# Picking the first pair's rows in one row of eight, and asking for four weight pieces ahead of the gate products

## The chip, the core and the metric

One core of a Trainium2 chip runs the whole program. The metric is the device time of one execution in microseconds, the median of three runs. Engines: TensorE (PE; its weight loads are shown as PEld), VectorE (DVE), ScalarE (ACT), GpSimd (POOL) and SyncE (SP), which only issues transfers.

## What is computed

A decoder layer for 512 tokens of 1024 channels in float32: three token mixers (pooling, latent attention, cross-attention into a memory), gated, projected and added to the residual, then a mixture of experts and a last norm. The change lies in the mixture of experts:

```
g_idx = argmax(h2 @ w_rg + b_rg)                 # 1 of 4 groups
top_p, top_i = top_k(softmax(e_logits[g_idx]), 2)  # 2 of its 8 experts
weights = p_g * top_p / sum(top_p)
for each expert e, on its tokens xb:
    a = silu(xb @ w_gate_e[e]) * (xb @ w_up_e[e])  # 1024 -> 256
    y = a @ w_down_e[e]                            # 256 -> 1024
out = x + sum over a token's experts of weight * y ; out = rms_norm(out)
```

Each of the 32 experts has 3.1 MB of weights, and all of them are read once.

## The kernel before

The first two thirds of the program (to about 527 us) compute the mixers, the projection and the router. Then the 32 experts are worked off as 16 pairs (`Pair`, `PP[0]` to `PP[15]`). A pair has 128 slots, 64 for each expert; `onehot` makes its matrix P (token by slot, a 1 where the token sits in the slot), and `by_slot` multiplies P with a few columns per token, which gives these columns by slot. With the token numbers that yields the row numbers for the gather (`place`, `fetch`: an indirect DMA on POOL from the copy `xd` of the rows in DRAM into `XG`, of which there are two, XB and a tile called y); with `INF` it yields the weights of the slots (`info`).

The rows of a pair are needed with channels on the partitions, as eight blocks k of 128 channels by 128 slots. For pairs 1 to 15 they are gathered and then turned (`turn_x`, four blocks at a time). The first pair doesn't wait for a gather: `pick_x` multiplies the rows in SBUF (`ACC`) with P, four matmuls a block, and ScalarE copies the block to SBUF with the norm's gain. In `up(k)` block k meets the gate and up weights of both experts (four passes on PE, 128x512 in the trace, into the bank `gu`); `turn` and `down` follow one pair later.

The order on every engine is the one in which the program is written; each pair goes through a list of steps. For the first pair that is `SEQ0`:

```
"X0 b1 X1 b2 X2 U0 X3 U1 X4 U2 X5 U3 X6 U4 X7 U5 j0 o U6 j1 x0 U7 L x1 j2 j f"
```

Xk is `pick_x(k)`; bn is the slot product with token numbers and the gather of pair n; Uk is `up(k)`; jn is `info` of pair n (without a number, of pair 3), o the `onehot` of pair 3, f its gather; xc is `turn_x(c)` of the next pair; L is told of below. Four blocks in a row share one PSUM bank (tag xe, two banks); the slot products have one bank (tag at).

Weights come in 192 pieces of 512 KB through a ring of 40 places made of tiles that earlier stages leave free (`place`, `load_piece`). After every second U, `used(2)` says that two places are free, and SP then issues the next two pieces (`load`); `down` frees four. SP issues in the order of the program, and a request waits until its place is free and until a transfer eight before it has landed. Places 36 to 39 of the ring are the tile `ac`, the place of `ACC`: x's rows lie there until the last pick. Their pieces (the down weights of pair 2) are left out by `load` and asked for in step L, behind U7. At pair 9 (`SC`) the rows, to which pairs 0 to 8 have added their results in DRAM (`xo`, indirect DMAs on POOL), are read back into SBUF (L1363), and later pairs add theirs there (`combine`, matmuls L1177 and additions L1179).

Of the kernel before, what the change touches and what calls it, by code (L numbers as in the profile page):

```python
# [9 lines left out]
F32 = mybir.dt.float32  # L10
# [3 lines left out]
AF = mybir.ActivationFunctionType  # L14
# [8 lines left out]
KD = 8  # L23
# [14 lines left out]
P_MIX, P_MEM, P_Q, P_KV, P_PS, P_GB, P_FFN, P_END = 0, 8, 16, 19, 21, 25, 49, 57  # L38
# [3 lines left out]
def trunk_and_moe(ctx, tc, a, out):  # L42
    nc = tc.nc
    v, s, g, pe = nc.vector, nc.scalar, nc.gpsimd, nc.tensor
# [34 lines left out]
    def nm(b):  # L79
        n[0] += 1  # L80
        return f"{b}{n[0]}"

    def at(dt=F32, shape=(128, 512)):
        return UA.tile(list(shape), dt, tag="u", name=nm("u"), bufs=8)
# [17 lines left out]
    def mt(dt=F32, shape=(128, 512)):  # L102
        return G2.tile(list(shape), dt, tag="m", name=nm("m"), bufs=6)
# [4 lines left out]
    def bank(p, tag, bufs, shape=(128, 512)):  # L108
        return p.tile(list(shape), F32, tag=tag, name=nm(tag), bufs=bufs)

    def mmb():
        return bank(PA, "mm", 4)

    K = cst.tile([128, C_END], F32, name="K")
    PR = cst.tile([128, P_END], F32, name="PR")
# [223 lines left out]
    ps = mmb()  # L339
# [157 lines left out]
    for h_ in range(XHEADS):  # L497
# [3 lines left out]
        ps = mmb()  # L501
        mm3(ps[:, :MEM], kterms(w, ms))
        tick()
        t = mt()
# [28 lines left out]
    for h_ in range(XHEADS):  # L533
# [22 lines left out]
        ps = mmb()  # L556
# [54 lines left out]
    scale = 192.0 ** -0.5  # L611
# [23 lines left out]
    for d in range(KD):  # L635
        w = WS.use("w_bpm", d)
        res = []
        for j, y in enumerate((yp, ym)):
            ps = mmb()
# [39 lines left out]
    def load_piece(i):  # L679
        e, c = pieces[i]  # L680
        ts = place(i)
        n_ = 2 // len(ts)
        for t in ts:
            if len(ts) == 2:
                t = t.unsqueeze(1)
            sync.dma_start(t, a["w_e"][e, :, c * T:(c + n_) * T].rearrange("p (k f) -> p k f", f=T))
            W[e][c:c + n_] = [t[:, j] for j in range(n_)]
            c += n_
# [12 lines left out]
    def used(n_):  # L701
        ring["used"] += n_
        load(max(min(ring["used"] + RING, 3 * RING - 4), ring["used"] + RING - 4))
# [96 lines left out]
    for h_ in range(HEADS):  # L800
        for op in SEQ:
            k, i = op[0], op[1:]
# [21 lines left out]
            elif k == "V" and h_ % 2:  # L824
                p = (h_ + 1) // 2
# [97 lines left out]
    def row_major():  # L923
        return W1.tile([128, 8, T], F32, tag="ac", name=nm("ACC"), bufs=1).rearrange("p (t a) b -> p t (a b)", t=4).rearrange("p t (a b) -> p t a b", b=128)

    ACC = row_major()
# [72 lines left out]
    L = R1[:, :, 0:36]  # L999
# [4 lines left out]
    def bc(x, *shape):  # L1004
        while len(x.shape) < len(shape):
            x = x.unsqueeze(len(x.shape))
        return x.broadcast_to(list(shape))
# [31 lines left out]
    tokr = cst.tile([128, 4, 2], F32R, name="tokr")  # L1039
# [12 lines left out]
    PC = Scope("pc", space=PSUM).p  # L1052
# [8 lines left out]
    def ut(shape, dt=F32):  # L1061
        return W1.tile(list(shape), dt, tag="e1", name=nm("u"), bufs=18) if extra[0] else at(dt, shape)

    class Pair:
# [25 lines left out]
        def pick_x(self, k):  # L1090

            if k % 4 == 0:
                self.xps = bank(PC, "xe", 2, (128, 4, 128))
                self.xe.append(ut((128, 4, 128)))
            for t in range(4):
                pe.matmul(self.xps[:, k % 4], lhsT=ACC[:, t, k], rhs=self.P[:, t].bitcast(F32), start=t == 0, stop=t == 3)
            s.activation(self.xe[-1][:, k % 4], self.xps[:, k % 4], AF.Copy, scale=PR[:, P_FFN + k:P_FFN + k + 1])

        def turn_x(self, c):
            ps = bank(PC, "xe", 2, (128, 4, 128))  # L1100
# [72 lines left out]
    def combine(i, q):  # L1173
        t, hs = i // 2, slice((i % 2) * 512, (i % 2) * 512 + 512)
        cb = bank(PC, "cb", 1) if i % 2 else bank(PC, "xe", 2)
        for j in range(2):
            pe.matmul(cb, lhsT=q.PT[:, t], rhs=q.y[j][:, hs], start=j == 0, stop=j == 1)  # L1177
        dst = ACC[:, t].rearrange("p a b -> p (a b)")[:, hs]
        v.tensor_tensor(dst, dst, cb, op=OP.add)  # L1179

    def pairs(x):
        return x.rearrange("p t (b a) -> p t a b", b=2)
# [5 lines left out]
    PP = [Pair(p, pairs(code)[:, :, p], None, scattered=p < SC) for p in range(NP)]  # L1188
    for q in PP[:3]:
        q.onehot()  # L1190


    v.tensor_reduce(sm[:, 6], t4, axis=AX, op=OP.add)
    v.scalar_tensor_tensor(sm[:, 9], sm[:, 8], 1.0, sm[:, 6], op0=OP.add, op1=OP.mult)
# [3 lines left out]
    v.tensor_tensor(t32, A1, bc(sm[:, 10], 128, 4, 32), op=OP.mult)  # L1198
    v.tensor_tensor(Wd, A2, bc(sm[:, 11], 128, 4, 32), op=OP.mult)
    v.tensor_tensor(Wd, Wd, t32, op=OP.add)  # L1200
    tok = K[:, C_TOKID:C_TOKID + 4]
    INF = cst.tile([128, 4, NE // 2, 8], F32R, name="INF")

# [9 lines left out]
    def tiles():  # L1213
        mps = bank(PC, "y", 2, (128, 32))
        for t in range(4):
            pe.matmul(mps, lhsT=KB[:, B_ONES:B_ONES + 128], rhs=Ab[:, t], start=t == 0, stop=t == 3)
        v.reduce_max(nt[:, 0:16], mps.rearrange("p (b a) -> p a b", b=2), axis=AX)
        v.reduce_max(nt[:, 16:17], nt[:, 0:16], axis=AX)
        v.tensor_scalar(flag, nt[:, 16:17], float(CAP), None, op0=OP.is_gt)
# [57 lines left out]

    SEQ0 = "X0 b1 X1 b2 X2 U0 X3 U1 X4 U2 X5 U3 X6 U4 X7 U5 j0 o U6 j1 x0 U7 L x1 j2 j f".split()  # L1280
    SEQM = "o U0 c U1 j c U2 c t c U3 x0 D n U4 w c U5 c x1 c U6 f c U7".split()
    SEQ14 = "U0 c U1 c U2 c t c U3 x0 D U4 w U5 c c x1 c c U6 c c U7 c c".split()
    SEQL = "t D U0 U1 U2 U3 I c c U4 s0 c c U5 s1 c c U6 s2 U7 r3 c c s3 r4 S0 S1 t S2 S3".split()
# [5 lines left out]
    def wide():  # L1289
        return W0.tile([128, 2, T], F32, tag="e0", name=nm("e"), bufs=6).rearrange("p a b -> p (a b)")  # L1290

    for p, q in enumerate(PP):
        q.wts = [W[2 * p], W[2 * p + 1]]
        last = p == NP - 1
        if p == NP - 2:
            gf = XG[0]
            g.dma_start(gf, a["final_g"].broadcast_to([128, D]))
        if last:

            q.rw = fs[:, 0, 3:4]  # L1300
            v.tensor_tensor(q.rw, q.rs, q.wt, op=OP.mult)
            junk, o = wide(), wide()
            ys = []
        for op in (SEQ0 if p == 0 else SEQL if last else SEQ14 if p == NP - 2 else SEQM):
            n_ = int(op[1]) if len(op) > 1 else p + 3
            if op[0] == "U":
                q.up(n_)
                if n_ % 2:
                    used(2)
            elif op == "c" and todo:  # L1310
                todo.pop(0)()
            elif op[0] == "X":
                q.pick_x(n_)
            elif op[0] == "b":
                PP[n_].fetch(PP[n_].by_slot(tokr, 2)[:, 0:1])
            elif op[0] == "x" and not last:
                PP[p + 1].turn_x(n_)
            elif op == "w" and SC <= p < NP - 1:
                q.where()
            elif op == "L":  # L1320
                PP[0].place(PP[0].it[:, 6:7])
                for i in range(RING - 4, RING):
                    load_piece(i)
            elif op == "n" and p == 1:
                tiles()
            elif op[0] in "ojf" and n_ < NP:
                if op[0] == "o":
                    PP[n_].onehot()
                if op[0] == "j":
                    PP[n_].info()  # L1330
                if op[0] == "f":
                    PP[n_].fetch(PP[n_].it[:, 6:7])
            elif op == "I":
                order.__exit__(None, None, None)
                with tc.If(nc.values_load(flag[0:1, 0:1], min_val=0, max_val=1) > 0):
                    extra[0] = True
                    overflow()
                    extra[0] = False
                order = tc.manual_schedule()
                order.__enter__()  # L1340
            elif op[0] == "s":
                s.activation(junk, tok_rows(n_), AF.Square, accum_out=fs[:, n_, 0:1])
            elif op[0] == "r":
                ts = slice(0, 3) if n_ == 3 else slice(3, 4)
                s.activation(fs[:, ts, 1], fs[:, ts, 0], AF.Sqrt, bias=eps[:, 0:1], scale=1.0 / D)
                if n_ == 4:
                    v.reciprocal(fs[:, 0:3, 2], fs[:, 0:3, 1])
            elif op[0] == "S":
                if n_ == 0:
                    ys += [bank(PC, "y", 2) for hf in range(2)]  # L1350
                for hf in range(2):
                    pe.matmul(ys[hf], lhsT=q.P[:, n_].bitcast(F32), rhs=tok_rows(n_)[:, hs[hf]], start=n_ == 0, stop=False)  # L1352
            elif op == "t" and last and ys:
                q.turn()
            elif op == "t":
                PP[p - 1].turn()
            elif op == "D":
                PP[p - 1].down()
                used(4)
                if p == SC:  # L1360
                    ACC = row_major()
                    for t in range(4):
                        g.dma_start(ACC[:, t].rearrange("p a b -> p (a b)"), xo[t * 128:(t + 1) * 128])  # L1363
                if p > SC:
                    todo += [lambda i=i, q=PP[p - 1]: combine(i, q) for i in range(8)]
# [9 lines left out]
    f = fs[:, 4]  # L1375
# [103 lines left out]
```

## Time and profile before

| | |
|---|---|
| median of 3 runs | 800.81 us (800.29 to 801.99) |
| the profiled execution, its own time | 801.2 us |
| its span (first to last instruction) | 799.4 us |
| mean granted clock of TensorE | 0.992 |
| PE busy | 775.8 us, 97% |
| transfers | 164.17 MB, 205 GB/s on average |

The profile is a list of what each engine did and when. The page divides the span into 40 slices of 20 us; the expert stage is slices 27 to 40. A busy share tells how much of a stretch an engine worked, an idle time in square brackets behind an instruction who ended the wait before it. The trace puts a matmul's line on PE (its duration holds the way through the array, so that neighbours overlap) and its weight load on PEld. A float32 product of the picks shows as two passes, so that a pick of four matmuls has eight loads; SPq and POOL DMA lines are the issuing of transfers, not their movement.

### The profile page before, as it was taken

What the parts mean: (1) busy time and instruction counts of PE and PEld (TensorE: products, weight loads), DVE (VectorE), ACT (ScalarE), POOL (GpSimd) and SP (SyncE); (2) the same over time, 40 slices, a digit from 0 to 9 for tenths busy, and PEclk for the clock granted to TensorE, in tenths of its full rate; (3) what the DMA queues carried; (4) which work ended last, traced back from release to release, by engine and by line L of the source; (5) the groups of instructions that cost most, each with busy time, mean ns of one, the idle gap of its engine ahead of it and who ended that gap; (6) DMA issues with size and microseconds to landing.
All of it is one profiled execution on the core that took longest, in us unless ns stands there. A gap on an engine that the chain in (4) does not pass through costs nothing. (4 is left out here: it accounts for less than half of the span.)

```text
span 799.4 us, 10154 instructions
## 1 busy us (share of the span) xinstructions
PE 775.8 (97%) x3743; PEld 523.8 (66%) x3743; DVE 366.3 (46%) x673; ACT 303.6 (38%) x623; POOL 277.1 (35%) x169
## 2 busy tenths in 40 slices
PE   7999999999999999999999999999999999999995
PEld 3778888888887888788888888854333333333432
DVE  5669684243446134677774433142212122454544
ACT  6254354343345544655653321122232223122223
POOL 3156676543241689522222924230212122000000
PEclk8999999999999999999999999999999999999998
DMA  6532333322221322211115379988999999999963
GB/s 220 186 106 106 106 106 132 132 80 80 80 79 43 110 89 82 64 47 57 54 54 211 132 277 342 374 289 307 392 378 383 402 367 388 408 372 390 409 264 121
DMA packets 53509, 164.17 MB, mean 205 GB/s; under 512 B 7906, under 2 KB 9058, under 8 KB 53456
## 3 DMA queue, kind: packets, MB, share of 16 engines
q1 hardware_dynamic: 46224, 149.14, 50.8%
q0 software_dynamic: 4640, 9.90, 3.9%
q10 hardware_dynamic: 2592, 4.46, 1.5%
q8 instruction: 30, 0.49, 0.3%
q14 instruction: 23, 0.19, 0.1%
HBM read 158.82 MB, written 11.53 MB: 213 GB/s over the span
## 5 line engine op out<-in xcount | busy, mean ns | idle before, releaser
L125 POOL TENSOR_TENSOR wl<-r,wh 128x1024 fp32r<-128x1024 f32 (+3 forms) x75 | 167.9, 2245 | 211.2 <-ACT wh L180 191.3
L180 ACT CAST wh<-r 128x1024 fp32r<-128x1024 f32 (+3 forms) x85 | 82.1, 972 | 31.8 <-PE mm L199 12.6
L1131 PE MATMUL gu<-e,u 128*64 128x512 f32 x336 | 88.5, 607 | 1.4 <-DMA e<-in_w_e 1.4
L198 PE MATMUL mm<-g,wh 128*128 128x512 f32 x180 | 71.9, 400 | 0.0
L199 PE MATMUL mm<-g,wh 128*128 128x512 f32 x180 | 70.2, 390 | 0.0
L1107 ACT ACTIVATE u<-xe,PR 128x128 f32<-128x128 f32 x120 | 34.3, 368 | 67.1 <-PE xe L1103 67.0
L471 PE MATMUL mm<-box,wh 128*128 128x512 f32 x144 | 56.8, 394 | 0.9 <-ACT wh L180 0.9
L472 PE MATMUL mm<-box,wh 128*128 128x512 f32 x144 | 56.2, 391 | 0.0
L201 PE MATMUL mm<-g,wl 128*128 128x512 f32 x180 | 52.6, 391 | 0.0
L1161 POOL DMA_INDIRECT xo<-y,ix x9 | 14.3, 1594 | 89.8 <-DVE ix L1082 79.7
L435 ACT ACTIVATE m<-s,st 128x256 f32<-128x256 f32 (+3 forms) x48 | 24.4, 509 | 54.5 <-DVE st L433 54.0
L1131 PEld LDWEIGHTS gu<-e,u 128*64 128x64 f32 x336 | 20.5, 135 | 33.7 <-issue 26.3
L1170 PE MATMUL y<-e,u 128*64 128x512 f32 x160 | 38.6, 600 | 0.6 <-DMA e<-in_w_e 0.6
L201 PEld LDWEIGHTS mm<-g,wl 128*128 128x128 f32 x180 | 33.8, 188 | 7.4 <-POOL wl L125 0.2
L198 PEld LDWEIGHTS mm<-g,wh 128*128 128x128 f32 x180 | 34.0, 189 | 6.4
L199 PEld LDWEIGHTS mm<-g,wh 128*128 128x128 f32 x180 | 33.9, 188 | 6.4
L476 PE MATMUL mm<-box,wl 128*128 128x512 f32 x144 | 36.6, 390 | 0.0
L198 PE MATMUL mm<-box,wh 128*128 128x512 f32 x78 | 31.7, 406 | 0.9 <-DVE g L283 0.9
L1157 DVE TENSOR_SCALAR y<-y,it 128x512 f32<-128x512 f32 x9 | 6.8, 751 | 54.1 <-PE y L1170 54.1
L471 PEld LDWEIGHTS mm<-box,wh 128*128 128x128 f32 x144 | 27.1, 188 | 6.7 <-ACT wh L180 1.3
L476 PEld LDWEIGHTS mm<-box,wl 128*128 128x128 f32 x144 | 27.0, 188 | 5.8
L472 PEld LDWEIGHTS mm<-box,wh 128*128 128x128 f32 x144 | 27.1, 188 | 5.3
(358 smaller groups left out, 1650.2 us busy)
## 6 DMA issues: line engine op xcount, KB each, us to landing
e<-in_w_e SPq DMA_DIRECT2D x124, 512.0 KB
r<-in_w_in SPq DMA_DIRECT2D x37, 512.0 KB
r<-in_w_e SPq DMA_DIRECT2D x15, 512.0 KB
wh<-in_w_e SPq DMA_DIRECT2D x15, 512.0 KB
wl<-in_w_e SPq DMA_DIRECT2D x15, 512.0 KB
m<-in_w_e SPq DMA_DIRECT2D x30, 256.0 KB
r<-in_w_bpm SPq DMA_DIRECT2D x8, 512.0 KB
r<-in_w_bl SPq DMA_DIRECT2D x8, 512.0 KB
```

The costliest lines, as they stand in the source:

```text
L125: eng.tensor_tensor(lo, x, hi.bitcast(F32), op=OP.subtract)
L180: s.copy(hi[:, :cols], r[:, :cols])
L198: pe.matmul(ps, lhsT=lh, rhs=rh, start=start and i == 0, stop=False)
L199: pe.matmul(ps, lhsT=lh, rhs=rl, start=False, stop=False)
L201: pe.matmul(ps, lhsT=ll, rhs=rh, start=False, stop=stop and i == m - 1)
L435: s.activation(P[:, :w], S[:, :w], AF.Exp, bias=st4[:, 0:1], accum_out=st4[:, 1:2])
L471: pe.matmul(ps, lhsT=lh, rhs=rh, start=k == 0, stop=False)
L472: pe.matmul(ps, lhsT=lh, rhs=rl, start=False, stop=False)
L476: pe.matmul(ps, lhsT=ll, rhs=rh, start=False, stop=k == KD - 1)
L1107: s.activation(x[:, j], ps[:, j], AF.Copy, scale=PR[:, k:k + 1])
L1131: pe.matmul(gu[r], lhsT=self.xe[k // 4][:, k % 4, r], rhs=self.wts[b][k], start=k == 0, stop=k == KD - 1)
L1170: pe.matmul(y[r], lhsT=self.aT[:, k, r], rhs=self.wts[b][8 + 2 * k + hf], start=k == 0 and not more, stop=k == 1)
```

## The change

All eight picks of the first pair stand in a row, ahead of the router's last sums, with one slot product (for pair 1) behind the first pick. Each block has a bank of its own, of the two with tag xe, in place of a quarter of one. The gather of pair 1 is issued from the index that is computed ahead of `INF`; that of pair 2 (b2) behind U0. Step L stands at the head of `SEQ0`, behind the last pick; what else it did, the row numbers of the first pair's slots, is now step p behind U7.

```diff
         def pick_x(self, k):
             if k % 4 == 0:
-                self.xps = bank(PC, "xe", 2, (128, 4, 128))
                 self.xe.append(ut((128, 4, 128)))
+            ps = bank(PC, "xe", 2, (128, 128))
             for t in range(4):
-                pe.matmul(self.xps[:, k % 4], lhsT=ACC[:, t, k], rhs=self.P[:, t].bitcast(F32), start=t == 0, stop=t == 3)
-            s.activation(self.xe[-1][:, k % 4], self.xps[:, k % 4], AF.Copy, scale=PR[:, P_FFN + k:P_FFN + k + 1])
+                pe.matmul(ps, lhsT=ACC[:, t, k], rhs=self.P[:, t].bitcast(F32), start=t == 0, stop=t == 3)
+            s.activation(self.xe[-1][:, k % 4], ps, AF.Copy, scale=PR[:, P_FFN + k:P_FFN + k + 1])
...
     for q in PP[:3]:
         q.onehot()
+    def first_fetch(p):
+        PP[p].fetch(PP[p].by_slot(tokr, 2)[:, 0:1])
+
+    PP[0].pick_x(0)
+    slot1 = PP[1].by_slot(tokr, 2)
+    for k in range(1, KD):
+        PP[0].pick_x(k)
...
     v.tensor_tensor(Wd, Wd, t32, op=OP.add)
+    PP[1].fetch(slot1[:, 0:1])
...
-    SEQ0 = "X0 b1 X1 b2 X2 U0 X3 U1 X4 U2 X5 U3 X6 U4 X7 U5 j0 o U6 j1 x0 U7 L x1 j2 j f".split()
+    SEQ0 = "L U0 b2 U1 U2 U3 U4 U5 j0 o U6 j1 x0 U7 p x1 j2 j f".split()
...
-            elif op[0] == "X":
-                q.pick_x(n_)
             elif op[0] == "b":
-                PP[n_].fetch(PP[n_].by_slot(tokr, 2)[:, 0:1])
+                first_fetch(n_)
...
+            elif op == "p":
+                PP[0].place(PP[0].it[:, 6:7])
             elif op == "L":
-                PP[0].place(PP[0].it[:, 6:7])
                 for i in range(RING - 4, RING):
                     load_piece(i)
```

On PE, from the first pick on, before (xe is the picks' bank, at the slot products' bank, gu the gate products' bank, e the weights; two gate matmuls are one step U):

```order
L1096 MATMUL xe_4685<-P_4662,ACC_4110 128x128 x4
L1077 MATMUL at_4692<-tokr,P_4664 128x2 x4
L1096 MATMUL xe_4685<-P_4662,ACC_4110 128x128 x4
L1077 MATMUL at_4707<-tokr,u_4666 128x2 x4
L1096 MATMUL xe_4685<-P_4662,ACC_4110 128x128 x4
L1131 MATMUL gu_4722<-e_3860,u_4686 64x512
L1131 MATMUL gu_4722<-e_3862,u_4686 64x512
L1096 MATMUL xe_4685<-P_4662,ACC_4110 128x128 x4
```

and after:

```order
L1096 MATMUL xe_4669<-P_4662,ACC_4110 128x128 x4
L1077 MATMUL at_4675<-tokr,P_4664 128x2 x4
L1096 MATMUL xe_4680<-P_4662,ACC_4110 128x128 x4
L1096 MATMUL xe_4686<-P_4662,ACC_4110 128x128 x4
L1096 MATMUL xe_4692<-P_4662,ACC_4110 128x128 x4
L1096 MATMUL xe_4699<-P_4662,ACC_4110 128x128 x4
L1096 MATMUL xe_4705<-P_4662,ACC_4110 128x128 x4
L1096 MATMUL xe_4711<-P_4662,ACC_4110 128x128 x4
L1096 MATMUL xe_4717<-P_4662,ACC_4110 128x128 x4
L1131 MATMUL gu_4750<-e_3860,u_4668 64x512
L1131 MATMUL gu_4750<-e_3862,u_4668 64x512
L1077 MATMUL at_4753<-tokr,u_4666 128x2 x4
```

The picks alternated with gate steps from the third on; now all eight stand ahead of the first step, each with a number of its own for its bank, and the second slot product has moved behind that step.

SP's requests for weights, from the last ones that are the same in both, before (ac is the place of x's rows):

```order
L686 DMA m_4534<-in_w_e 128x512
L686 DMA e_4732<-in_w_e 128x1024
L686 DMA e_4734<-in_w_e 128x1024
L686 DMA e_4752<-in_w_e 128x1024
L686 DMA e_4754<-in_w_e 128x1024
L686 DMA e_4770<-in_w_e 128x1024
L686 DMA e_4772<-in_w_e 128x1024
L686 DMA e_4813<-in_w_e 128x1024
L686 DMA e_4815<-in_w_e 128x1024
L686 DMA ac_4819<-in_w_e 128x1024 x4
```

and after:

```order
L686 DMA m_4534<-in_w_e 128x512
L686 DMA ac_4745<-in_w_e 128x1024 x4
L686 DMA e_4765<-in_w_e 128x1024
L686 DMA e_4767<-in_w_e 128x1024
L686 DMA e_4773<-in_w_e 128x1024
L686 DMA e_4775<-in_w_e 128x1024
```

The four pieces for ac have moved ahead of the eight that the first pair's gate steps make room for. All SP requests behind them are the same.

## Rows read from the trace of the kernel before

**Rows 1.** The page, 40 slices of 20 us: busy tenths of PE and of the DMA engines.

```profile
PE   7999999999999999999999999999999999999995
DMA  6532333322221322211115379988999999999963
```

**Rows 2.** Busy time by stretch of the expert stage: length, then PE, PEld, DVE, ACT and POOL, granted clock, DMA share, GB/s.

```profile
537.00:556.00 19.00, 18.68 (x106) 9.33 (x104) 4.62 (x25) 5.28 (x17) 0.99 (x1) 1.00 0.85 295
556.00:672.00 116.00, 115.13 (x554) 40.93 (x550) 23.19 (x77) 33.26 (x95) 22.66 (x17) 1.00 1.02 384
672.00:697.00 25.00, 22.47 (x85) 7.56 (x82) 9.34 (x19) 4.51 (x12) 4.33 (x6) 1.00 1.03 409
697.00:760.00 63.00, 63.00 (x269) 23.54 (x267) 30.75 (x54) 17.18 (x46) 2.54 (x3) 1.00 1.01 392
```

**Rows 3.** SyncE: what its weight requests (L686) waited for, in 533 to 556 (first row) and in 560 to 680 (two rows): us in total, times, longest; and its requests in order of time.

```profile
SPq L686 <- PE gu L1131: 16.2, 6, 4.3
...
SPq L686 <- DMA e<-in_w_e: 55.3, 50, 2.2
...
SPq L686 <- PE gu L1131: 2.4, 9, 0.4
...
535.42 12.80 SPq L686 DMA_DIRECT2D e<-in_w_e  x8
548.45 1.93 SPq L686 DMA_DIRECT2D ac<-in_w_e  x4
```

**Rows 4.** From the first pick to j0 in order of time (start, us, engine, line, operation, in brackets the idle time before and what ended it): weight loads of PE, one matmul line, lines of ScalarE, DVE and POOL; last the group of the picks' loads with its busy time and the mean of one in ns.

```profile
526.69 0.97 PEld L1096 LDWEIGHTS xe<-P,ACC 128*128 128x128 f32 x8 [0.52 <-DVE P L1071]
527.58 0.53 PEld L1077 LDWEIGHTS at<-tokr,P 128*128 128x128 f32 x4
527.89 0.37 ACT L1097 ACTIVATE u<-xe,PR 128x128 f32<-128x128 f32 x1 [2.48 <-PE xe L1096]
528.31 0.97 PEld L1096 LDWEIGHTS xe<-P,ACC 128*128 128x128 f32 x8 [0.20 <-ACT u L1097]
530.38 0.22 DVE L1209 CAST INF<-K 128x64 fp32r<-128x64 f32 x1
530.68 0.61 PE L1077 MATMUL at<-tokr,u 128*128 128x2 f32 x4 [1.22 <-DVE ix L1082]
531.12 0.97 PEld L1096 LDWEIGHTS xe<-P,ACC 128*128 128x128 f32 x8
...
532.99 1.04 POOL L1087 DMA_INDIRECT y<-xd,ix  x1 [0.30 <-issue]
533.23 0.97 PEld L1096 LDWEIGHTS xe<-P,ACC 128*128 128x128 f32 x8 [0.81 <-issue]
534.32 0.20 PEld L1131 LDWEIGHTS gu<-e,u 128*64 128x64 f32 x4
...
543.71 0.52 PEld L1077 LDWEIGHTS at<-INF,P 128*128 128x128 f32 x4 [0.81 <-issue]
544.25 0.20 PEld L1131 LDWEIGHTS gu<-e,u 128*64 128x64 f32 x4
...
L1096 PEld LDWEIGHTS xe<-P,ACC 128*128 128x128 f32 x64 | 7.7, 191 | 4.8 <-ACT u L1097 2.6 <-issue 1.6 <-DVE P L1071 0.5
```

**Rows 5.** PE in a later pair, where nothing is late: four gate steps and what follows them, the sixteen down matmuls and what follows them.

```profile
587.08 3.65 PE L1131 MATMUL gu<-e,u 128*64 128x512 f32 x16
590.83 0.58 PE L1077 MATMUL at<-INF,P 128*128 128x8 f32 x4
...
594.31 3.65 PE L1170 MATMUL y<-e,u 128*64 128x512 f32 x16
597.79 1.89 PE L1131 MATMUL gu<-e,u 128*64 128x512 f32 x8
```

**Rows 6.** The second gathered pair's rows (tile y) as PE first reads them, and the time from issue to landing of the transfers of xd.

```profile
553.98 0.66 PE L1103 MATMUL xe<-K,y 128*128 128x128 f32 x4
...
DMA to landing us min/median/max: 3.5/8.3/15.5
```

**Rows 7.** PE in 672 to 697, the groups with a wait before them and those on either side.

```profile
673.05 1.08 PE L1170 MATMUL y<-e,u 128*64 128x512 f32 x4
...
677.61 0.59 PE L1131 MATMUL gu<-e,u 128*64 128x512 f32 x1
...
682.73 0.73 PE L1177 MATMUL xe<-y,u 128*128 128x512 f32 x2 [0.48 <-DVE ACC L1179]
...
685.07 1.93 PE L1131 MATMUL gu<-e,u 128*64 128x512 f32 x6
688.15 1.07 PE L1131 MATMUL gu<-e,u 128*64 128x512 f32 x2 [1.15 <-DMA e<-in_w_e]
...
691.93 1.07 PE L1131 MATMUL gu<-e,u 128*64 128x512 f32 x2
693.27 1.07 PE L1131 MATMUL gu<-e,u 128*64 128x512 f32 x2 [0.27 <-DMA e<-in_w_e]
```

**Rows 8.** The rows that are read back: their issue on POOL, and DVE's additions to them.

```profile
674.60 2.22 POOL L1363 DMA_DIRECT2D ACC<-xo  x4 [7.88 <-DMA e<-in_w_e]
...
681.99 0.69 DVE L1179 TENSOR_TENSOR ACC<-ACC,xe 128x512 f32<-128x512 f32 x1 [0.99 <-DMA e<-in_w_e]
...
684.57 0.69 DVE L1179 TENSOR_TENSOR ACC<-ACC,xe 128x512 f32<-128x512 f32 x1 [1.29 <-DMA ACC<-xo]
```

## The prediction

> **What bounds the kernel now.** I read the page first, then the stretches, then single engines. The page shows PE busy in nearly every slice, and the DMA engines at 8 tenths in slices 27 and 28 (520 to 560 us) and at 9, full, from slice 29 nearly to the end [rows 1]. So the expert stage, from 527 us on, has two limits that lie close together, and the table by stretch says which holds where [rows 2]: in 537 to 556 the DMA engines work at 0.85 and move 295 GB/s while PE works; in 556 to 672 they are full (1.02, 384 GB/s) and PE too (115.1 of 116 us); in 672 to 697 they are full (409 GB/s) and PE is busy for only 22.5 of 25 us; in 697 to 760 PE is busy for all 63 us. Transfers fall behind PE for 116 us, PE waits for them once, and after that PE alone sets the pace. SyncE's waits say the same [rows 3]: up to 556 it waits for PE to give places back (16.2 us), from 560 to 680 almost only for earlier transfers (55.3 us for e alone, against 2.4 us for the gate products). A saving on PE at the start is therefore worth nothing by itself if the weights don't come earlier as well; both have to be counted.
>
> **PE's side.** The stretch from the first pick (526.69) to the product j0 (543.71) takes 17.02 us [rows 4]. It holds 8 picks (X), 6 gate steps (U) and 2 slot products (b).
> - A pick's eight weight loads span 0.97 us and one lasts 0.191, so they follow each other every (0.97 - 0.19) / 7 = 0.111 us: a pick among its like takes 8 x 0.111 = 0.89, which is also what lies between the first pick and the slot product behind it (526.69 to 527.58). Its bound from above is the whole span, 0.97. From 533.23 to 543.71 five pairs of pick and gate step take 10.48, 2.10 a pair, 1.09 of it for the pick (533.23 to 534.32) and 1.00 for the step; sixteen gate matmuls in a row, four steps, take 3.75 (587.08 to 590.83 [rows 5]), 0.94 a step.
> - After: 8 picks 7.12; slot product in the row 0.44 (530.68 to 531.12); six steps 5.64; slot product between steps 0.54 (543.71 to 544.25); one change from picks to steps 0.20 (1.09 - 0.89). Sum 13.94. **PE reaches j0 3.1 us earlier** (2.5 at 0.97 a pick). Two things go: the hole of 529 to 531, where the second slot product waited 1.22 us for DVE to read the first one out of their one bank, and the price of alternating, 2.10 - 0.89 - 0.94 = 0.27 for each of six pairs.
> - The wait of the second pick for ScalarE's copy of the first (528.26 to 528.31) goes with the common bank. With two banks a pick waits for the copy of the pick two before: it ends 1.57 after that pick's first load (526.69 to 528.26) [rows 4], and two picks take 1.78. So no pick should wait.
> - The pieces of the new helper cost nothing on their own: the index of the second pair is computed before six INF instructions in place of behind them, INF is done at 530.6 and first used by j0. The second pair's gather is issued about 1 us earlier, the third's later: its product runs behind U0 at 535.4, so its issue moves from 532.99 to about 537. It is read in the second pair's x0, at 553.98 now and 550.9 after [rows 6]. That leaves 14 us; issue to landing was 3.5 to 15.5, median 8.3. I take no wait.
>
> **The transfers' side.** In 537 to 556 they move 295 x 19 = 5.6 MB. At the 384 GB/s of 556 to 672 that is 14.6 us of 19, at the 409 GB/s of 672 to 697 13.7, and by busy share 0.85 / 1.02 x 19 = 15.8 [rows 2]. So 3.2 to 5.3 us of transfer time stand empty, because SyncE asks only as fast as gate steps free two places: 535.42, then some 4 us apart, and the four pieces for x's places only at 548.45 [rows 3]. After, x is read for the last time by the eighth pick, which ends at 526.69 + 7.12 + 0.44 = 534.25; the four pieces (2.1 MB, 5.5 us at 384 GB/s) are asked for then, pairs follow at about 536.9, 538.8, 540.6 and 544.2, and 14 pieces then keep the engines full until about 555. I take 4.4 (the rate of the stretch that follows, with the same gathers and scatters in it), and 1.1 for the earlier start (535.42 to 534.3), less 0.5 for a gap that may open near 557: **the transfers run 5.0 us ahead**, with bounds 3.2 and 6.4. What has to hold is that SyncE never waits for a place again before 672; rows 3 give 0.4 us as its longest wait for a gate product there.
>
> The Trainium skill, "DMA: Bandwidth & Descriptors", section Specifications, gives about 358 GB/s as the HBM limit of one core; by it the 5.6 MB would be 15.6 us and the lead 4.0. The 409 GB/s of rows 2 lie above it, so the rows decide.
>
> **Where the two meet.** In 672 to 697 PE loses, against its own undisturbed groups [rows 5], 1.08 us in the down products (673.05 to 677.61, 4.56 against 3.48), 1.67 at 685.07 (six matmuls, 1.41, next at 688.15) and 0.87 at 691.93 (two, 0.47, next at 693.27) [rows 7]. With PE 3.1 and the weights 5.0 ahead, the first goes. It is not kept: at 682.73 PE waits for DVE's first addition to the rows that were read back (read back at 674.60 to 676.82, added from 681.99) [rows 7, 8], a chain that begins with the down products of the pair before, so it moves by PE's 3.1 alone. Behind it the other two waits can go: 3.1 + 1.67 + 0.87 = 5.6 is what PE could gain, 5.0 is what the weights allow. **Smaller of the two: 5.0.** From 697 on PE is busy throughout and carries it to the end; the last waits there (a branch, a copy) move along.
>
> Sum: the profiled execution's own 801.2, less 5.0, is **796.2**. The median of three runs, 800.81, is 0.4 lower; I stay with the sum and let the range take that.
>
> **Rivals.**
> 1. PE's part alone: the lead of the transfers is lost on the way (SyncE waits for places, or the additions to the read-back rows hold PE later too). 801.2 - 3.1 = 798.1. For it: the additions of [rows 8] wait for their transfer a second time, until 684.57. Against: [rows 3]. Chance 0.20.
> 2. No change: the transfers of 537 to 556 can't be packed tighter, the weights come when they came, and PE waits 3.1 longer at 673 to 693. 801. For it: the busy share, 0.85, is nearer to full than the 295 GB/s. Against: 1.02 and 384 GB/s directly behind. The same end comes if a pick's weight load does not run beside the matmul before it: 64 loads at their mean of 0.191 [rows 4] are 12.2 us, PE reaches j0 2.0 late, the four pieces are asked for at 539.3, which uses up the lead of 5.0, and the shorter waits at 685 and 693 take that up. The Trainium skill, "TensorE: Matmul & The Clock Gate", in "What overlaps and what doesn't" of Part 3, lets a weight load run beside a matmul only where their row groups differ, and all of these use all rows. By that rule the loads would not overlap; the trace disagrees, eight loads of 0.191 in 0.97. Chance 0.12.
> 3. Slower: picks held by ScalarE. First pick to second takes 1.62 now, with the copy's end the last thing waited for, second to third 2.81, with a wait for DVE [rows 4]. If banks don't alternate in fact, eight picks take 13 to 22 us. Each microsecond that the row ends after 534.25 postpones the four pieces, and the lead is gone 5.0 later, at 539.25, a pitch of 1.51. At 1.62 the row ends at 540.1 and the weights come 0.8 late, 802.0; at 2.0 it ends at 543.1 and they come 3.9 late, 805.1. Chance 0.05.
> 4. More than forecast: the weights 6 us ahead, and PE takes its whole 5.6: 795.6. Chance 0.07.
>
> **How the numbers follow.** The forecast has 0.56. 0.2% is 1.6 us, what a measurement of this kernel can tell. Faster by more: forecast, 1 and 4, 0.83, less 0.01 for a lead that ends short of it: 0.82. Within: rival 2 and that, 0.13. Slower: 0.05. Range: rival 4, 0.4 for the median and 0.4 for the spread of runs at the low end, 794.8; at the high end rival 1 and half of the way to no change, 799.6.
>
> **What would show it.** In the profile after: eight picks in a row with loads 0.97 us long and about 0.89 apart, no wait of PE on the pick's line; j0 near 540.6; the ac requests near 534.3 and the DMA engines above 1.0 from 537 to 556 (about 380 GB/s); PE busy for over 24 us of the 25 before 694, the remaining wait at the additions. Wrong would be: picks over 1.1 apart (rival 3), DMA share of 537 to 556 still near 0.85, or PE's waits for e near 680 as long as before or longer (rival 2).

## The result, and the profile after

The changed kernel takes 796.88 us, the median of 4 runs (796.18 to 797.78), against 800.62 us of the kernel before (now 4 runs, 800.29 to 801.99): 0.9947 of its time, 95% interval 0.9929 to 0.9965. The forecast was 796.2. The profiled execution took 797.49 us with a span of 795.7 and a mean granted clock of 0.997.

The page's slices, in the form of [rows 1]:

```profile
PE   6999999999999999999999999999999999899995
DMA  6533234322220422211215379989999999999963
```

In slice 28 (540 to 560 us) the DMA engines now work at 9 tenths, before at 8. By stretch, in the form of [rows 2]:

```profile
537.00:556.00 19.00, 18.68 (x98) 7.77 (x98) 4.78 (x26) 4.86 (x15) 2.03 (x2) 1.00 1.01 380
672.00:697.00 25.00, 22.97 (x90) 8.20 (x90) 9.30 (x19) 5.27 (x14) 4.31 (x6) 1.00 1.03 409
```

The first stretch moves 380 GB/s in place of 295. In 672 to 697 PE is busy for 22.97 us in place of 22.47; the two other stretches are nearly as they were (384 and 390 GB/s, PE busy for 115.12 of 116 and for all 63 us). The picks and j0, weight loads of PE in order of time, against [rows 4]:

```profile
527.72 0.97 PEld L1096 LDWEIGHTS xe<-P,ACC 128*128 128x128 f32 x8 [0.52 <-DVE P L1071]
...
529.06 6.33 PEld L1096 LDWEIGHTS xe<-P,ACC 128*128 128x128 f32 x56
535.51 0.20 PEld L1131 LDWEIGHTS gu<-e,u 128*64 128x64 f32 x4
...
541.50 0.52 PEld L1077 LDWEIGHTS at<-INF,P 128*128 128x128 f32 x4 [0.81 <-issue]
```

Seven picks, 56 loads, run without a wait in 6.45 us (529.06 to 535.51), 0.92 each. j0 (541.50) comes 13.78 us after the first pick; before it was 17.02. The first pick itself stands 1.03 us later than in the profile of before (527.72 against 526.69), behind code that is the same in both. In all profiles of this study it lies between 525.40 and 527.72, so from here on times are counted **from the first pick**.

SyncE's requests for weights in order of time, against [rows 3]:

```profile
535.65 1.76 SPq L686 DMA_DIRECT2D ac<-in_w_e  x4
538.16 20.84 SPq L686 DMA_DIRECT2D e<-in_w_e  x18
```

and what they waited for in 560 to 680:

```profile
SPq L686 <- DMA e<-in_w_e: 53.1, 47, 2.0
...
SPq L686 <- PE gu L1131: 2.6, 9, 0.4
```

The four pieces for x's places are asked for 7.93 us after the first pick (before 21.76), and the others follow behind earlier transfers, not behind gate steps. PE where it lost time before, against [rows 7]:

```profile
670.84 3.69 PE L1170 MATMUL y<-e,u 128*64 128x512 f32 x15
...
675.75 0.73 PE L1177 MATMUL xe<-y,u 128*128 128x512 f32 x2
...
679.93 0.73 PE L1177 MATMUL xe<-y,u 128*128 128x512 f32 x2 [1.35 <-DVE ACC L1179]
...
682.27 2.00 PE L1131 MATMUL gu<-e,u 128*64 128x512 f32 x8
684.20 0.73 PE L1177 MATMUL xe<-y,u 128*128 128x512 f32 x2
...
688.32 1.07 PE L1131 MATMUL gu<-e,u 128*64 128x512 f32 x2 [0.27 <-DMA e<-in_w_e]
...
692.27 1.46 PE L1170 MATMUL y<-e,u 128*64 128x512 f32 x4
693.92 1.07 PE L1170 MATMUL y<-e,u 128*64 128x512 f32 x2 [0.20 <-DMA e<-in_w_e]
695.21 2.36 PE L1170 MATMUL y<-e,u 128*64 128x512 f32 x9 [0.21 <-DMA e<-in_w_e]
...
698.78 0.73 PE L1177 MATMUL xe<-y,u 128*128 128x512 f32 x2
...
783.56 3.65 PE L1170 MATMUL y<-e,u 128*64 128x512 f32 x16
```

The down products at 670.84 run without an idle time, and so do the eight gate matmuls at 682.27. What is left is the wait for the additions (1.35, before 0.48), one short wait for a weight at 688.32, as before, and **new** ones in the down products at 692.27: from there to the next product for the additions (698.78) PE takes 6.51, and before it took 5.23, by these rows of its PE line:

```profile
697.21 4.01 PE L1170 MATMUL y<-e,u 128*64 128x512 f32 x15
...
702.44 0.73 PE L1177 MATMUL xe<-y,u 128*128 128x512 f32 x2
```

So late weights cost 1.28 more there than before. The read-back and DVE's additions, against [rows 8]. First POOL, with the last scatter of results ahead of the read-back, which the read-back waits for:

```profile
662.91 1.59 POOL L1161 DMA_INDIRECT xo<-y,ix  x1 [10.18 <-DMA e<-in_w_e]
672.18 2.21 POOL L1371 DMA_DIRECT2D ACC<-xo  x4 [7.67 <-DMA e<-in_w_e]
```

before, the scatter stood here:

```profile
665.13 1.59 POOL L1161 DMA_INDIRECT xo<-y,ix  x1 [10.19 <-DMA e<-in_w_e]
```

Then DVE:

```profile
679.19 0.69 DVE L1179 TENSOR_TENSOR ACC<-ACC,xe 128x512 f32<-128x512 f32 x1 [1.86 <-DMA e<-in_w_e]
```

Counted from the first pick, the scatter is issued 3.25 us earlier than before (135.19 against 138.44), which is PE's lead, and the addition starts 3.83 earlier (151.47 against 155.30).

The last sixteen down matmuls before the end (783.56) stand 255.84 us after the first pick. Before, it was 260.54, by this row of its PE line:

```profile
787.23 3.65 PE L1170 MATMUL y<-e,u 128*64 128x512 f32 x16
```

So the change gives **4.70 us** from the first pick on, less 1.03 by which that pick was late: 3.67, and the two profiled executions differ by 801.2 - 797.49 = 3.71.

### The profile page after: what moved, and what is told of

The parts are those of the page before. It is cut to its first block, busy times and chain, and to the rows that moved or that the text cites. A ratio compares the mean times of both kernels' runs of the same rounds, so it can differ in the third digit from the quotient of the medians.

```text
span 795.7 us, 10156 instructions
## 1 busy us (share of the span) xinstructions
PE 772.1 (97%) x3743; PEld 523.5 (66%) x3743; DVE 366.2 (46%) x673; ACT 303.2 (38%) x623; POOL 277.3 (35%) x169
## 5 line engine op out<-in xcount | busy, mean ns | idle before, releaser
L1131 PE MATMUL gu<-e,u 128*64 128x512 f32 x336 | 86.3, 606 | 0.3 <-DMA e<-in_w_e 0.3
```

Of the source, the lines that this page charges most:

```text
L1131: pe.matmul(gu[r], lhsT=self.xe[k // 4][:, k % 4, r], rhs=self.wts[b][k], start=k == 0, stop=k == KD - 1)
```

## Experiments

The theory: the time follows the lead of the weights, that is, the time by which the transfers run ahead of before, as long as PE can use it. The rival: PE's earlier arrival at j0 is the gain, the requests only go with it. For each run I read three numbers: j0 after the first pick (PE's lead), the GB/s moved from 8 to 29 us after the first pick (the weights' lead), and the last down matmuls after the first pick (the gain). Before moved 276 GB/s in that window:

```profile
534.69:555.69 21.00, 20.68 (x116) 10.40 (x114) 4.62 (x25) 5.62 (x19) 0.99 (x1) 1.00 0.81 276
```

and the change 362:

```profile
535.72:556.72 21.00, 20.68 (x110) 8.66 (x108) 5.35 (x27) 5.12 (x16) 2.03 (x2) 1.00 0.97 362
```

At the 384 GB/s of the stretch that follows, the extra bytes are a lead of (362 - 276) x 21 / 384 = 4.70 us. All runs, in us:

| kernel | PE's lead at j0 | GB/s, 8 to 29 us | lead of the weights | gain, first pick to last down | median (before) | ratio, 95% interval |
|---|---|---|---|---|---|---|
| the change | 3.24 | 362 | 4.70 | 4.70 | 796.88 (800.62) | 0.9947, 0.9929 to 0.9965 |
| after_again | 3.24 | 361 | 4.65 | 3.91 | 796.3 (801.44) | 0.9928, 0.9901 to 0.9956 |
| e1_row_late_request | 3.24 | 306 | 1.64 | 1.37 | 799.17 (801.29) | 0.997, 0.9955 to 0.9984 |
| e2_alternating_early_request | -0.01 | 315 | 2.13 | 1.63 | 798.56 (801.29) | 0.9971, 0.9953 to 0.999 |
| e3_row_shared_banks | -0.65 | 286 | 0.55 | 0.87 | 799.94 (801.29) | 0.9985, 0.9974 to 0.9996 |
| e5_extra_transfers | 3.25 | 362 | -0.80, see below | -0.73 | 801.46 (801.29) | 1.0005, 0.999 to 1.0021 |
| e4_places_freed_by_quarter | 3.24 | 388 | 6.13 | 6.50 | 794.11 (801.44) | 0.9906, 0.9879 to 0.9933 |
| e6_quarter_and_later_additions | 3.24 | 385 | 5.96 | 6.29 | 794.57 (801.44) | 0.9905, 0.9879 to 0.9932 |

The gain stands within 0.8 us of the weights' lead in every row. It follows PE's lead in none of e1, e2, e3 and e5. The table doesn't hang on where the window ends: counted to 140 us after the first pick (before 368 GB/s, the change 382), the leads are 4.8, 4.5, 1.4, 2.1, 0.7, -1.4, 6.2 and 5.5 in the order of the rows, again within 0.8 us of the gains. The medians, which hold the part ahead of the first pick as well, differ from those before by 3.7, 5.1, 2.1, 2.7, 1.4, -0.2, 7.3 and 6.9 in the same order.

### The row without the early request

Against the change:

```diff
-    SEQ0 = "L U0 b2 U1 U2 U3 U4 U5 j0 o U6 j1 x0 U7 p x1 j2 j f".split()
+    SEQ0 = "U0 b2 U1 U2 U3 U4 U5 j0 o U6 j1 x0 U7 L p x1 j2 j f".split()
```

> The changed kernel with one part undone: the four pieces for x's places are asked for behind U7 again, as before; the eight picks stay in a row. Theory (two limits: PE's lead and the weights' lead, the smaller one counts from 697 us on): j0 stands 13.8 us after the first pick as in the changed kernel, but the requests for the four pieces come some 10 us later, the weights are ahead by 3.2 us only, the lead of PE's own steps, and PE waits for weights near 690 again. From the first pick to the last down products 257.3 us (before 260.5, changed 255.8), time about 798.4. Rival (PE's steps alone make the gain): 255.8, time about 796.9 as in the changed kernel. Rival (the early request alone makes it): 259.5 or more, time 799.5 or more.

PE has its whole lead of 3.24 us, and the gain is 1.37. The first request for e is now 10.44 us after the first pick (before 8.73), since the picks stand ahead of the first gate steps, and the ac request 18.51 after it (before 21.76):

```profile
535.84 7.85 SPq L686 DMA_DIRECT2D e<-in_w_e  x8
543.91 1.75 SPq L686 DMA_DIRECT2D ac<-in_w_e  x4
```

The waits for weights come back in PE's line:

```profile
677.15 1.07 PE L1131 MATMUL gu<-e,u 128*64 128x512 f32 x2 [1.21 <-DMA e<-in_w_e]
...
687.26 1.07 PE L1131 MATMUL gu<-e,u 128*64 128x512 f32 x2 [1.29 <-DMA e<-in_w_e]
```

My own theory's number, 257.3 us to the last down, missed (259.17): it counted the ac request as 3.2 earlier and left out that the eight requests ahead of it began later. Counted by bytes the lead is 1.64, near the 1.37 measured. PE's arrival alone isn't the gain: 1.37 of 4.70 is left, by the medians 2.1 where the change has 3.7 and 5.1.

### The early request without the row

Against the kernel before, with the place of the first pair's slots as a step p of its own:

```diff
-    SEQ0 = "X0 b1 X1 b2 X2 U0 X3 U1 X4 U2 X5 U3 X6 U4 X7 U5 j0 o U6 j1 x0 U7 L x1 j2 j f".split()
+    SEQ0 = "X0 b1 X1 b2 X2 U0 X3 U1 X4 U2 X5 U3 X6 U4 X7 L U5 j0 o U6 j1 x0 U7 p x1 j2 j f".split()
...
-            elif op == "L":
+            elif op == "p":
                 PP[0].place(PP[0].it[:, 6:7])
+            elif op == "L":
                 for i in range(RING - 4, RING):
```

> The kernel before with one part of the change: picks and gate steps alternate as before, the four pieces for x's places are asked for right behind the last pick, 5.7 us earlier than before. Theory (two limits): j0 stays 17.0 us after the first pick, the weights are ahead by 2 to 2.8 us, PE gains nothing up to the additions to the read-back rows at 682, and then gets up to 2.5 us back out of its two waits for weights behind them. From the first pick to the last down products 258.2 us (before 260.5), time about 798.3. Rival (PE's steps alone make the gain): 260.5, time 800.6. Rival (the early request alone makes all of the gain): 256.5, time 796.9.

The ac request stands 16.16 us after the first pick, 5.60 earlier than before:

```profile
541.78 1.75 SPq L686 DMA_DIRECT2D ac<-in_w_e  x4
```

PE has no lead at all (j0 after 17.03), and still 1.63 us are gained. PE's wait for the additions has grown with what the weights no longer cost:

```profile
681.07 0.73 PE L1177 MATMUL xe<-y,u 128*128 128x512 f32 x2 [1.51 <-DVE ACC L1179]
```

Each half alone leaves requests that wait for gate steps (DMA share of the window 0.85 in e1 and 0.89 in e2, 0.97 in the change): only both together fill the DMA engines. Whether the halves' gains make less than the whole is not shown: by the profiles they are 3.00 together, against 4.70 and 3.91 of the change, by the medians 4.9 against 3.7 and 5.1.

### The row with the shared banks

Against the change:

```diff
             if k % 4 == 0:
+                self.xps = bank(PC, "xe", 2, (128, 4, 128))
                 self.xe.append(ut((128, 4, 128)))
-            ps = bank(PC, "xe", 2, (128, 128))
+            ps = self.xps[:, k % 4]
```

> The changed kernel with four picks in one bank as before, in the row of eight. Theory: each pick waits for ScalarE's copy of the one before in its bank, 1.5 to 1.6 us from pick to pick in place of 0.9, the row ends near 12 us after its start in place of 7.6, j0 some 18 us after the first pick, the request for the four pieces comes 4 to 5 us later than in the changed kernel and the weights' lead is nearly gone: from the first pick to the last down products 259.5 to 261 us, time 800 to 801.5. Rival (the banks don't matter): the row stays at 0.9 a pick, 255.8 us, time 796.9.

The picks, weight loads of PE:

```profile
527.38 0.97 PEld L1097 LDWEIGHTS xe<-P,ACC 128*128 128x128 f32 x8 [0.20 <-ACT u L1098]
529.00 0.97 PEld L1097 LDWEIGHTS xe<-P,ACC 128*128 128x128 f32 x8 [0.65 <-ACT u L1098]
...
536.35 0.97 PEld L1097 LDWEIGHTS xe<-P,ACC 128*128 128x128 f32 x8 [0.65 <-ACT u L1098]
```

All but the fifth, the first in the second bank, wait for ScalarE's copy of the one before, 1.62 apart (527.38 to 529.00), and the eighth comes 10.59 us after the first (525.76), in the change 6.86 us after it (529.06 and six times 0.92, less 527.72). So a bank for each block is what lets the row run; without it PE reaches j0 0.65 later than before. The kernel is none the less not slower than before (0.9985, interval to 0.9996), and the ac request still comes 11.82 us after the first pick, 9.94 earlier than before:

```profile
537.58 1.75 SPq L686 DMA_DIRECT2D ac<-in_w_e  x4
```

### Four transfers more

Against the change, four transfers of 512 KB that nobody reads, one ahead of each of pieces 60 to 63, from DRAM to DRAM:

```diff
+    extra_d = dram.tile([4, 128, 2 * T], F32, name="extra_d")
...
     def load_piece(i):
         e, c = pieces[i]
+        if 60 <= i < 64:
+            sync.dma_start(extra_d[i - 60], a["w_e"][e, :, 0:2 * T])
```

> The changed kernel with four more transfers of 512 KB in the queue of weights, from DRAM to a scratch in DRAM that nothing reads, each ahead of one of the pieces 60 to 63 (asked for near 560 us). They cost the DMA engines some 5.5 us (2.1 MB at 384 GB/s) and no engine anything else. Theory (the weights set the end of the waits of PE near 690): PE waits that much longer there and the time is 4 to 6 us longer than the changed kernel's, 801 to 803. Rival (PE's steps set the time and the weights have room): within 1 us of the changed kernel's 796.9.

2.1 MB at 384 GB/s are 5.5 us, an estimate from the rate of 556 to 672. The first pick to the last down takes 261.27, 5.43 more than in the change and 4.64 more than in its second profile (below); the lead of 4.70 less 5.5 is the -0.80 of the table. PE's lead is untouched, and what takes it back are waits for weights, for instance:

```profile
680.69 1.07 PE L1135 MATMUL gu<-e,u 128*64 128x512 f32 x2 [1.49 <-DMA e<-in_w_e]
...
690.08 1.07 PE L1135 MATMUL gu<-e,u 128*64 128x512 f32 x2 [0.58 <-DMA e<-in_w_e]
```

So a microsecond of transfer time in the full stretch costs about a microsecond, as far as two profiles can tell.

### More lead: places freed by quarter

If bytes moved early are what pays, asking still earlier must pay more. Against the change, the last four picks go through four banks at once, token block by token block, so that a quarter of x's rows is read for the last time sooner; pieces 36 to 39 go into the tile of the rows itself, so that each waits only for the matmuls that read its quarter:

```diff
+        def pick_rest(self):
+            ps = [bank(PC, "y", 2, (128, 128)), bank(PC, "y", 2, (128, 128)), bank(PC, "cb", 1, (128, 128)), bank(PC, "gu", 2, (128, 128))]
+            self.xe.append(ut((128, 4, 128)))
+            for t in range(4):
+                for j in range(4):
+                    pe.matmul(ps[j], lhsT=ACC[:, t, 4 + j], rhs=self.P[:, t].bitcast(F32), start=t == 0, stop=t == 3)
...
-            if j == 36:
+            if i == 36:
+                ring["ac"] = ring["raw"]
+            elif j == 36:
...
-    for k in range(1, KD):
+    for k in range(1, 4):
         PP[0].pick_x(k)
+    PP[0].pick_rest()
```

> The changed kernel, with the last four picks turned inside out: blocks 4 to 7 stand in four banks at once (of the tags y, cb and gu, free at that time) and are summed over the four quarters of the rows one quarter at a time, so that a quarter of x's place is free about 4.9, 5.8, 6.7 and 7.6 us after the first pick, and its piece is asked for then (in the changed kernel all four at 7.9). Same matmuls on PE. Theory (the weights' lead sets the time; it was 4.7 us in the changed kernel by the bytes moved up to 29 us after the first pick): another 2 to 3 us of transfer time are filled, PE's waits for weights near 688 and 694 (0.9 and 1.2 us) go, its wait for the additions to the read-back rows stays: from the first pick to the last down products 253.8 us (changed 255.8), time 2 us below the changed kernel's. Rival (PE's steps set the time): 255.8, the changed kernel's time.

The four pieces are asked for one by one from 5.27 us after the first pick on (the change 7.93):

```profile
531.27 2.96 SPq L688 DMA_DIRECT2D ACC<-in_w_e  x4
```

The gain is 6.50, the median 794.11 against 796.3 of the change on the same chip (6 runs each, 793.33 to 796.0 and 795.23 to 798.3): faster than the kernel before and than the change. No wait for a weight is left on PE: from 540 to 784 us it waits for nothing longer than 0.5 us but the additions, and the clock falls behind that wait. The last two rows show a group of down products without late weights and the product that follows, 4.44 later:

```profile
678.33 0.73 PE L1189 MATMUL xe<-y,u 128*128 128x512 f32 x2 [1.93 <-DVE ACC L1191]
...
684.09 0.73 PE L1189 MATMUL xe<-y,u 128*128 128x512 f32 x2
...
690.81 3.65 PE L1182 MATMUL y<-e,u 128*64 128x512 f32 x16
...
695.25 0.73 PE L1189 MATMUL xe<-y,u 128*128 128x512 f32 x2
```

by stretch:

```profile
678.30:680.00 1.70, 1.67 (x6) 0.49 (x6) 0.57 (x1) 0.00 (x0) 0.00 (x0) 0.94 1.04 410
680.00:682.00 2.00, 2.00 (x6) 0.80 (x6) 1.33 (x3) 0.00 (x0) 0.00 (x0) 0.50 1.01 401
```

From the product at 678.33 to the one at 684.09 PE takes 5.76; in the change the same stretch (679.93 to 684.20) takes 4.27 at a granted clock of 1.00. So the wait of 1.93 was followed by 1.49 more, at the lower clock.

### More lead, and the additions later

Against the version by quarter, in the pair behind the read-back:

```diff
+    SEQ10 = "o U0 c U1 j c U2 c t c U3 x0 D n U4 w U5 c x1 c U6 c f U7 c".split()
...
-        for op in (SEQ0 if p == 0 else SEQL if last else SEQ14 if p == NP - 2 else SEQM):
+        for op in (SEQ0 if p == 0 else SEQL if last else SEQ14 if p == NP - 2 else SEQ10 if p == SC + 1 else SEQM):
```

> The kernel with quarters of x's place, and in the one pair behind the read-back of the rows the steps that add the pair before are put one gate step later, so that DVE's first addition, which waits for the read-back, holds PE less. Theory: with the weights ahead by 6.7 us or more, PE's next limit is that wait (1.4 us in the changed kernel); it shrinks by about 0.9, and the time is 0.5 to 1 us below the kernel with quarters alone. Rival (the weights are used up again by then): the same as with quarters alone.

The wait for the additions is shorter, 1.48, and the clock stays at 1.00, but PE then waits for gathered rows (0.32) and for weights again:

```profile
678.93 0.73 PE L1189 MATMUL xe<-y,u 128*128 128x512 f32 x2 [1.48 <-DVE ACC L1191]
...
688.81 0.66 PE L1115 MATMUL xe<-K,y 128*128 128x128 f32 x4 [0.32 <-DMA y<-xd,ix]
...
690.98 1.07 PE L1182 MATMUL y<-e,u 128*64 128x512 f32 x2 [0.50 <-DMA e<-in_w_e]
```

The gain is 6.29, no more than without the later additions. PE stood 7.50 us ahead of before at these down products (689.40, 163.02 after the first pick, against 170.52), and the late weights took it down to the 6.29. At this lead both limits lie within a fraction of a microsecond of each other.

### The change once more

> The changed kernel itself, on the same chip as the two that build on it. Theory: j0 13.8 us after the first pick and the last down products 255.8 us after it again; ratio to before 0.9945, as first measured.

796.3 us beside the kernel before at 801.44 (11 runs), 0.9928. From first pick to last down 256.63, 0.79 more than in the first profile with the same j0 (13.78) and nearly the same bytes (361 GB/s). That is how far two profiles of one kernel differ here, and smaller differences in the table say nothing. The waits differ as well:

```profile
678.50 0.73 PE L1177 MATMUL xe<-y,u 128*128 128x512 f32 x2 [0.75 <-DVE ACC L1179]
...
683.17 1.07 PE L1131 MATMUL gu<-e,u 128*64 128x512 f32 x2 [0.40 <-DMA e<-in_w_e]
```

Here the wait for the additions is 0.75, not 1.35, and part of the wait for a weight that was gone in the first profile is back. Which wait shrinks by how much is thus a reading of one profile.

## Why the prediction was right

**The path.** It named the transfers as what decides, and that is shown: e1 keeps all of PE's lead and loses more than half of the gain, e2 gains without any lead of PE, e3 with PE late is not slower than before, e5 loses what the added transfers take, e4 gains more with more bytes moved early.

**PE's side: 3.1 forecast, 3.24 measured.** A pick 0.92 (0.89 forecast), none held by its copy. The Trainium skill, "TensorE: Matmul & The Clock Gate", "What overlaps and what doesn't" in Part 3, would have had the loads not run beside matmuls that use the same rows. The trace disagrees: 56 loads of 0.192 us mean, 10.8 us in sum, span 6.33 us. The third pair's gather moved as said (6.30 to 10.37 after the first pick), the second's by 0.3 in place of 1, and PE did not wait for what they brought.

**The weights' side: 5.0 forecast, 4.70 measured by bytes.** 380 GB/s in 537 to 556 against some 380 forecast. The start is 0.8 earlier (8.73 to 7.93 after the first pick), where the sum had 1.1: the row took 7.79 (527.72 to 535.51), not 7.56, and the request went out 0.14 behind it. The gap of 0.5 that was taken off for 557 did not open: the DMA share is 1.02 in 555 to 557 and 1.05 in 557 to 559. So the packing itself gave 3.9, not 4.4. A likely part of the difference is the start: in 535 to 537, around the request, the share is only 0.36. The Trainium skill, "DMA: Bandwidth & Descriptors", Specifications, would have made the lead 4.0, an estimate by its 358 GB/s for one core. This trace (380 to 409) and e4's 388 over 21 us lie above that figure. The same page of the Trainium skill, in its Bandwidth section under Measured, has up to 425 GB/s for one core while its neighbour is idle. With that the 380 to 409 here agree.

**Where the two meet.** "Smaller of the two" held, and the place shows it: before the down products at 692.27 PE stands 5.97 us ahead of before (692.27 - 527.72 = 164.55, against 170.52 for the same group, at 697.21, before), and the late weights there take it down to the 4.70 that stay. But PE's term, 5.6, was too low, because its waits were priced too low. In the undisturbed stretches the products of a pair's two experts run side by side, as these rows of before show, where their weights have two names:

```profile
709.88 0.64 PE L1131 MATMUL gu<-r,u 128*64 128x512 f32 x1
709.89 0.64 PE L1131 MATMUL gu<-wh,u 128*64 128x512 f32 x1
```

When one expert's weight is late, the other's products run alone, and the late ones alone behind them. So the wait at 688.15 costs its idle time of 1.15 and the 1.00 that the last two matmuls take: from 685.07 to 689.15 PE needs 4.08, and undisturbed 1.93 (682.27 to 684.20 in the change), 2.15 more, where the prediction had 1.67. In the same way the wait before 693.27 cost 1.33 (691.93 to the product at 694.27 is 2.34, four gate matmuls undisturbed 1.01), not 0.87. The first down products cost 1.92 (673.05 to the product at 679.41 is 6.36, in e4 4.44 again), not 1.08. The second ones, where the prediction saw PE busy throughout, cost 0.79 (5.23 against e4's 4.44), with no idle time at all.

With these prices PE could have gained 3.83 + 2.15 + 1.33 + 0.79 = 8.1, an estimate from these rows. What it did gain up to 692.27, in the first profile, is j0's 3.24, 1.45 of the first down products (4.91 now, 670.84 to 675.75), the 2.15, less 0.87 by which the wait for the additions grew: 5.97. In e4, where no weight is late, all four are gained, and 3.24 + 1.92 + 2.15 + 1.33 + 0.79, less 1.45 for the longer wait and 1.49 for the clock, is 6.49 of the 6.50 measured. The time came out right because the smaller term, the weights' 5.0, was off by 0.3 alone. That the larger error in PE's term didn't show is partly luck: at a lead of 6 the 5.6 would have capped the forecast wrongly, as e4's 6.50 shows. Against the profiled execution's 797.49 the forecast of 796.2 is 1.3 low, of which 1.03 is the later first pick, which no term of the sum held.

The chain through the additions was read rightly as one that moves with PE. The scatter moved by PE's 3.25, and the rest of the 3.83 is transfers that landed sooner. Over the runs the first addition starts 151.5 to 151.8 us after the first pick in the change (both profiles), e4 and e6, whose weights lead by 4.65 to 6.13, and 154.7 to 155.9 in before, e2 and e3, where PE has no lead.

**What it said would be seen, and wasn't.** PE busy for over 24 of the 25 us before 694: it was 23.18 in 669 to 694 and 22.97 in 672 to 697. The waits did not go, they moved: in the first profile the wait at 688.15 went, that before 693.27 stayed (688.32 now), and new ones came behind 692.27; in the second profile 0.40 of the former is left. What counts is when the last late weight lets PE through, not how the waits ahead of it share the time.

**The rivals.** PE's part alone (798.1) is refuted by e1: PE's lead without the weights' gives 1.37, and the change gives more than 3.1 in both profiles. No change (801) would have needed transfers that can't be packed tighter; 380 GB/s refutes it. Picks held by ScalarE didn't happen in the change. In e3, which brings that about, the request for the four pieces comes 3.89 us later than in the change (11.82 against 7.93) and the weights' lead is 4.15 smaller (0.55 against 4.70): the prediction's price, a microsecond of lead for each microsecond of delay, holds about. Its 802.0 for a pitch of 1.62 didn't come because the row was shorter than eight such pitches and a slot product: the fifth pick has the second bank free, and the eighth comes 10.59 us after the first. The case of more (795.6) wanted the weights 6 us ahead, which the change doesn't reach; e4 does, with 794.11.

**Left open.** How long the read-back can be put off without weights becoming late, that is, whether both limits can be lowered together: e6 tried one order alone. That PE's cap in e4 is its chain through the additions is read from rows, not tested by a kernel in which only that chain is shorter.

## What to carry to other kernels

Where transfers are full for a long stretch and the compute waits for them once at its end, what is worth moving is the point at which requests start to flow: count the bytes that a change brings forward, divide by the rate of the full stretch, and cap it with what the compute could gain. Price a late weight by the way to the next group that all need, not by the idle time: products that would have run side by side run one after the other. Look at what holds a buffer, and read it for the last time early: here eight reads in a row let 2.1 MB be asked for 14 us sooner. Count the requests behind the moved one as well, since a row of compute put ahead of the first release delays those (e1).

## What the runs showed of the hardware that was not expected

- **The clock falls behind a short wait.** In e4 PE waited 1.93 us for the additions, and the granted clock of the next stretches was 0.94, then 0.50 (1.2 of 2.4 GHz), with 1.49 us lost behind the wait; in e3, after a wait of 1.92 at the same place, it fell to 0.50 as well (684 to 686). After 1.51 (e2), 1.48 (e6) and 1.35 (the change) it stayed at 1.00. The wait in e3:

```profile
682.36 0.73 PE L1178 MATMUL xe<-y,u 128*128 128x512 f32 x2 [1.92 <-DVE ACC L1180]
```

- **A late weight costs more than its idle time.** Products of 64 columns of the two experts start 0.01 us apart and run side by side, eight gate matmuls in 1.93 us. Two that are left behind a wait take 1.00 by themselves, in the kernel before (688.15 to 689.15) and in the change (688.32 to 689.33), where two of eight would take 0.48.
- **The part ahead of the change varies.** The first pick lies between 525.40 and 527.72 us after the span's start in the profiles, with the same code before it: as much as half of the gain, which is why times were counted from it.
